# A FiLM layer on one core: slab 0 stored in five parts and loaded in two, and a small write of zeros left out

## The chip, the cores and the metric

The kernel runs on one core of a Trainium2 chip. The metric is device time in microseconds (us), the median of several runs; the kernel before takes 84.38 us (three runs, 84.28 to 84.4). A profile shows one execution. Its "span" runs from the first to the last instruction of the program, and its own time is a little longer than its span.

## The reference

```python
batch, seq, dim = 32, 512, 256
cond_dim = 64
...
    gamma = conditioning @ gamma_proj
    beta = conditioning @ beta_proj

    return (x * (1 + gamma[:, None, :]) + beta[:, None, :]).astype(np.float32)
```

All is float32. x and the output have 32 x 512 rows of 256 values, 1 KB a row and 16 MB each (16.78 million bytes). Every batch element has one row of gamma and one of beta, which are used for its 512 rows.

## The kernel before

**Tiling.** The 16384 rows are cut into four slabs of 4096 rows (SLABS, L29). In a slab each of the 128 partitions holds 32 rows that follow one another in memory (ROWS, L32), so a partition's share of a slab is one run of 32 KB, and 16 partitions share one batch element (REP). All four slabs fit in SBUF at once (tiles xs0 to xs3, L62), and nothing is loaded twice or waits for a buffer.

**Loads.** SyncE (SP) issues them all (L66): slab 0 in four DMAs of 8 rows (LOADS, L38), each of which moves 8 KB per partition, slabs 1 to 3 in one DMA each, 32 KB per partition. ScalarE (ACT) issues the small ones: conditioning (L49), then a write of zeros, then gamma_proj and beta_proj (L57, L58) into the even and odd rows of one tile, gbproj.

**The write of zeros.** POOL fills a tile of 16 rows with zeros (L52), and ACT issues one DMA (L54) which writes them to rows 0, 1024, 2048 and so on of the output: one row in each MB. The stores of the results write over them later.

**The coefficients.** VectorE widens conditioning into two tiles (L83, L84); TensorE multiplies each by an identity matrix that repeats every batch element 16 times (L74, L86), which transposes it; VectorE copies the result out of PSUM (L89). For each slab two matmuls with gbproj (L96) give gamma and beta for all partitions in PSUM (gb_p), and ACT copies them to SBUF (gb_s, L100 and L103), adding the 1 to gamma. VectorE reads them from PSUM, POOL, from SBUF.

**The arithmetic.** The loop (L110 to L127) goes over slabs and over two groups of 16 rows in each (GROUP). In a group VectorE takes the first 11 rows of a partition (ON_DVE) and POOL the other 5. Each makes one multiplication and one addition in place (L118 and L121 on VectorE, L120 and L122 on POOL).

**The stores.** ACT issues them (L126). STORES (L39) lists the rows up to which a store reaches: slab 0 in two halves of 16 rows, the others whole. The inner loop (L124) issues, behind each group, every store that ends in that group.

**The order.** The framework makes the semaphores and keeps each engine's instructions in an order of its own that follows the program. Loads stand on SP's queue (q1 in the profile), stores and the small DMAs on ACT's (q10). Both queues run on the same 16 DMA engines. Each DMA reports its end on one of the completion semaphores.

Of the kernel before, what the change touches and what calls it, by code (L numbers as in the profile page):

```python
# [2 lines left out]

# [5 lines left out]


@with_exitstack
def kernel(
    ctx: ExitStack,
    tc: tile.TileContext,
    x: bass.AP,
    conditioning: bass.AP,
    gamma_proj: bass.AP,
    beta_proj: bass.AP,
    out: bass.AP,  # L20
):
    nc = tc.nc
    f32 = mybir.dt.float32
    ALU = mybir.AluOpType

    batch, seq, dim = x.shape
    cond_dim = conditioning.shape[1]
    P = 128
    SLABS = 4  # L29
    BS = batch // SLABS  # L30
    REP = P // BS
    ROWS = BS * seq // P  # L32
    assert SLABS * BS == batch and REP * BS == P and ROWS * REP == seq

    x_v = x.flatten_outer_dims().rearrange("(s p r) d -> s p r d", s=SLABS, p=P)
    o_v = out.flatten_outer_dims().rearrange("(s p r) d -> s p r d", s=SLABS, p=P)

    LOADS = {0: [8, 8, 8, 8]}  # L38
    STORES = {0: (16, 32), 1: (32,), 2: (32,), 3: (32,)}  # L39
    GROUP = 16  # L40
    ON_DVE = 11

    consts = ctx.enter_context(tc.tile_pool(name="consts", bufs=1))
    xpool = ctx.enter_context(tc.tile_pool(name="xpool", bufs=1))
    psum = ctx.enter_context(tc.tile_pool(name="psum", bufs=1, space=bass.MemoryType.PSUM))


    cond_s = consts.tile([batch, cond_dim], f32)
    nc.scalar.dma_start(out=cond_s, in_=conditioning)  # L49

    zero = consts.tile([16, dim], f32)
    nc.gpsimd.memset(zero, 0.0)  # L52
    o_f = out.flatten_outer_dims()
    nc.scalar.dma_start(out=o_f.rearrange("(a b) d -> a b d", a=16)[:, 0, :], in_=zero)  # L54

    gbproj = consts.tile([2 * cond_dim, dim], f32)
    nc.scalar.dma_start(out=gbproj[0::2, :], in_=gamma_proj)  # L57
    nc.scalar.dma_start(out=gbproj[1::2, :], in_=beta_proj)  # L58

    slabs = []  # L60
    for s in range(SLABS):
        xs = xpool.tile([P, ROWS, dim], f32, name=f"xs{s}")  # L62
        slabs.append(xs)
        r = 0
        for n in LOADS.get(s, [ROWS]):
            nc.sync.dma_start(out=xs[:, r : r + n, :], in_=x_v[s, :, r : r + n, :])  # L66
            r += n
        assert r == ROWS


    ident = consts.tile([batch, batch], f32)
    make_identity(nc, ident)
    rident = consts.tile([batch, batch * REP], f32)
    nc.vector.tensor_copy(  # L74
        out=rident.rearrange("p (b g) -> p b g", g=REP),
        in_=ident.to_broadcast([batch, batch, REP]),
    )


    cond_T = []  # L80
    for h in range(2):
        wide = consts.tile([batch, cond_dim, 2], f32, name=f"wide{h}")
        nc.vector.memset(wide, 0.0)  # L83
        nc.vector.tensor_copy(out=wide[:, :, h], in_=cond_s)  # L84
        t_p = psum.tile([2 * cond_dim, batch * REP], f32, name=f"cond_T_p{h}")
        nc.tensor.matmul(t_p, lhsT=wide.rearrange("b k h -> b (k h)"), rhs=rident,  # L86
                         start=True, stop=True)
        t_s = consts.tile([2 * cond_dim, batch * REP], f32, name=f"cond_T{h}")
        nc.vector.tensor_copy(out=t_s, in_=t_p)  # L89
        cond_T.append(t_s)  # L90

    gb_p, gb_s = [], []
    for s in range(SLABS):
        p_t = psum.tile([P, 2 * dim], f32, name=f"gb_p{s}")
        for h in range(2):
            nc.tensor.matmul(p_t[:, h * dim : (h + 1) * dim],  # L96
                             lhsT=cond_T[h][:, s * P : (s + 1) * P], rhs=gbproj,
                             start=True, stop=True)
        s_t = consts.tile([P, 2 * dim], f32, name=f"gb_s{s}")
        nc.scalar.activation(out=s_t[:, :dim], in_=p_t[:, :dim],  # L100
                             func=mybir.ActivationFunctionType.Identity,
                             bias=1.0, scale=1.0)
        nc.scalar.copy(out=s_t[:, dim:], in_=p_t[:, dim:])  # L103
        gb_p.append(p_t)
        gb_s.append(s_t)

    def rows(t, n):
        return bass.AP(tensor=t.tensor, offset=t.offset, ap=[t.ap[0], [0, n], t.ap[1]])

    for s in range(SLABS):  # L110
        xs = slabs[s]
        g_p, b_p = gb_p[s][:, :dim], gb_p[s][:, dim:]
        g_s, b_s = gb_s[s][:, :dim], gb_s[s][:, dim:]
        for r0 in range(0, ROWS, GROUP):
            v = xs[:, r0 : r0 + ON_DVE, :]
            w = xs[:, r0 + ON_DVE : r0 + GROUP, :]
            nv, nw = ON_DVE, GROUP - ON_DVE
            nc.vector.scalar_tensor_tensor(out=v, in0=rows(g_p, nv), scalar=1.0, in1=v,  # L118
                                           op0=ALU.add, op1=ALU.mult)
            nc.gpsimd.tensor_tensor(out=w, in0=w, in1=rows(g_s, nw), op=ALU.mult)  # L120
            nc.vector.tensor_add(out=v, in0=v, in1=rows(b_p, nv))  # L121
            nc.gpsimd.tensor_tensor(out=w, in0=w, in1=rows(b_s, nw), op=ALU.add)  # L122

            for e0, e1 in zip((0,) + STORES[s], STORES[s]):  # L124
                if r0 < e1 <= r0 + GROUP:
                    nc.scalar.dma_start(out=o_v[s, :, e0:e1, :], in_=xs[:, e0:e1, :])  # L126
        assert STORES[s][-1] == ROWS  # L127


# [1 line left out]
_INS = ['x', 'conditioning', 'gamma_proj', 'beta_proj']  # L131
_OUTS = [((32, 512, 256), 'float32')]


# [23 lines left out]
```

## Time and profile before

| what | us |
|---|---|
| median of 3 runs | 84.38 |
| the profiled execution | 84.28 |
| its span | 82.5 |
| VectorE busy | 51.2 |
| POOL busy | 46.5 |
| TensorE busy | 9.0 |
| DMA queue q1 (loads), share of 16 engines' span | 48.7% |
| DMA queue q10 (stores and small DMAs), the same | 47.8% |

The DMAs of x, from the trace: when each was issued, and when the last of its 16 engines reported its end.

| DMA | issued | landed |
|---|---|---|
| slab 0, load, rows 0, 8, 16, 24 on | 0.75, 1.17, 1.64, 2.11 | 5.7, 8.4, 10.9, 13.4 |
| slab 1, load | 4.10 | 23.1 |
| slab 2, load | 6.35 | 36.9 |
| slab 3, load | 9.94 | 51.4 |
| slab 0, store, rows 0 to 15 | 22.10 | 40.5 |
| slab 0, store, rows 16 to 31 | 26.09 | 52.6 |
| slab 1, store | 38.34 | 62.3 |
| slab 2, store | 50.58 | 72.0 |
| slab 3, store | 63.93 | 81.7 |

How to read it: a busy engine is not yet the one that bounds the time. The time from a DMA's issue to its landing holds its stand in the queue as well as its transfer. The profile's slices, each a fortieth of the span, show in tenths how busy an engine was. The trace also has a record of each DMA packet, with its queue, size, start and duration; some records of the small end markers are doubled.

### The profile page before, as it was taken

The numbers are of one execution on the slowest core, as the hardware profiler recorded it, in microseconds if no ns is written. First come the engines' busy times: TensorE is split into PE (matmuls) and PEld (weight loads), VectorE is DVE, ScalarE is ACT, GpSimd is POOL, SyncE is SP. The second block draws the span as 40 slices with busy tenths as digits, with TensorE's granted clock in tenths as the row PEclk, the third lists the DMA queues.
The fourth block names the chain that finished last, engine by engine and source line by source line (L and its number), as shares of the span: only waits on it lengthen the run. The fifth ranks groups of instructions, "written<-read, shape, count | busy, mean of one in ns | idle before, by whom it ended". The sixth has DMA issues, their size and how long they took to land.

```text
span 82.5 us, 179 instructions
## 1 busy us (share of the span) xinstructions
PE 9.0 (11%) x20; PEld 5.2 (6%) x20; DVE 51.2 (62%) x23; ACT 3.8 (5%) x9; POOL 46.5 (56%) x23
## 2 busy tenths in 40 slices
PE   0069399300000000000000000000000000000000
PEld 0031178100000000000000000000000000000000
DVE  1023303999999999999999995999999000000000
ACT  0500005600000000000000000000000000000000
POOL 3000004999999999969999940999995000000000
PEclk9999999998555555555555555555555555555555
DMA  3799999989979999999899988979997995998890
GB/s 52 298 425 419 427 437 560 413 350 508 477 302 413 477 477 397 381 493 397 350 413 461 556 381 350 540 334 429 508 445 318 508 508 254 508 508 381 381 508 0
DMA packets 1968, 33.71 MB, mean 409 GB/s; under 512 B 288, under 2 KB 432, under 8 KB 432
## 3 DMA queue, kind: packets, MB, share of 16 engines
q1 hardware_dynamic: 1008, 16.78, 48.7%
q10 hardware_dynamic: 960, 16.93, 47.8%
HBM read 16.92 MB, written 16.79 MB: 409 GB/s over the span
## 4 chain that ended last, share of the span: by engine, by line
DMA 60%; DVE 15%; ACTq 1%; issue 1%; POOL 0%; DVEq 0%; POOLq 0%
DMA xs<-in_x_dram 50%; DMA gbproj<-in_beta_proj_dram 9%; DVE xs L121 7%; DVE xs L118 7%; ACTq L57 1%; ACTq L54 0%; POOL ident masks.py:199 0%; POOL ident masks.py:197 0%; POOL zero L52 0%; DVEq L118 0%; POOLq L142 0%
## 5 line engine op out<-in xcount | busy, mean ns | idle before, releaser
L120 POOL TENSOR_TENSOR xs<-xs,gb_s 128x1280 f32<-128x1280 f32 x8 | 23.0, 2897 | 15.9 <-ACT gb_s L100 12.1
L118 DVE SCALAR_TENSOR_TENSOR xs<-gb_p,xs 128x2816 f32<-128x2816 f32 x8 | 24.7, 3085 | 5.3 <-ACT gb_s L103 4.3
L121 DVE TENSOR_TENSOR xs<-xs,gb_p 128x2816 f32<-128x2816 f32 x8 | 24.7, 3087 | 0.3
L122 POOL TENSOR_TENSOR xs<-xs,gb_s 128x1280 f32<-128x1280 f32 x8 | 23.0, 2898 | 0.0
L96 PE MATMUL gb_p<-gbproj,cond_T 128*128 128x256 f32 x16 | 5.2, 494 | 1.4 <-DMA gbproj<-in_beta_proj_dram 1.4
L86 PE MATMUL cond_T_p<-rident,wide 32*128 32x512 f32 x4 | 3.8, 1096 | 4.9 <-DVE rident L74 4.9
L96 PEld LDWEIGHTS gb_p<-gbproj,cond_T 128*128 128x128 f32 x16 | 4.0, 261 | 3.7 <-DVE cond_T L89 3.0
L89 DVE COPY cond_T<-cond_T_p 128x512 f32<-128x512 f32 x2 | 1.4, 692 | 3.2 <-PE cond_T_p L86 3.2
L84 DVE COPY wide<-cond_s 32x64 f32<-32x64 f32 x2 | 0.3, 181 | 3.0 <-DMA cond_s<-in_conditioning_dram 3.0
L100 ACT ACTIVATE gb_s<-gb_p 128x256 f32<-128x256 f32 x4 | 1.5, 383 | 9.2 <-PE gb_p L96 9.2
L86 PEld LDWEIGHTS cond_T_p<-rident,wide 32*128 32x128 f32 x4 | 1.2, 318 | 5.9 <-DVE rident L74 4.8
L103 ACT COPY gb_s<-gb_p 128x256 f32<-128x256 f32 x4 | 1.5, 367 | 0.0
L100 ACT ACT_TABLE_LOAD x1 | 1.3, 1283 | 2.9 <-issue 2.9
L83 DVE MEMSET wide<- 32x128 f32 x2 | 0.3, 165 | 0.8 <-PEq L142 0.8
L52 POOL MEMSET zero<- 16x256 f32 x1 | 0.3, 301 | 0.3 <-POOLq L142 0.3
L74 DVE COPY rident<-ident 32x512 f32<-32x512 f32 x1 | 0.4, 407 | 0.0
masks.py:199 POOL TENSOR_SCALAR_AFFINE_SELECT ident<-ident 32x32 f32<-32x32 f32 x1 | 0.2, 202 | 0.1
L142 POOL MEMSET const-float32-0.0<- 128x1 f32 x1 | 0.1, 103 | 0.2 <-issue 0.2
masks.py:197 POOL MEMSET ident<- 32x32 f32 x1 | 0.1, 114 | 0.0
L142 POOL MEMSET const-bfloat16-1.0<- 128x1 bf16 x1 | 0.1, 111 | 0.0
L142 POOL MEMSET const-uint8-127<- 128x1 uint8 x1 | 0.1, 111 | 0.0
L142 POOL MEMSET const-float32-1.0<- 128x1 f32 x1 | 0.1, 108 | 0.0
## 6 DMA issues: line engine op xcount, KB each, us to landing
xs<-in_x_dram SPq DMA_DIRECT2D x3, 4096.0 KB, 30.5
out_dram<-xs ACTq DMA_DIRECT2D x3, 4096.0 KB, 21.4
xs<-in_x_dram SPq DMA_DIRECT2D x4, 1024.0 KB, 8.3
out_dram<-xs ACTq DMA_DIRECT2D x2, 2048.0 KB, 22.5
gbproj<-in_gamma_proj_dram ACTq DMA_DIRECT2D x1, 64.0 KB, 6.8
gbproj<-in_beta_proj_dram ACTq DMA_DIRECT2D x1, 64.0 KB, 7.7
cond_s<-in_conditioning_dram ACTq DMA_DIRECT2D x1, 8.0 KB, 3.3
out_dram<-zero ACTq DMA_DIRECT2D x1, 16.0 KB, 5.1
```

What stands on the lines that cost most here:

```text
L57: nc.scalar.dma_start(out=gbproj[0::2, :], in_=gamma_proj)
L74: nc.vector.tensor_copy(out=rident.rearrange("p (b g) -> p b g", g=REP), in_=ident.to_broadcast([batch, batch, REP]),)
L86: nc.tensor.matmul(t_p, lhsT=wide.rearrange("b k h -> b (k h)"), rhs=rident, start=True, stop=True)
L89: nc.vector.tensor_copy(out=t_s, in_=t_p)
L96: nc.tensor.matmul(p_t[:, h * dim : (h + 1) * dim], lhsT=cond_T[h][:, s * P : (s + 1) * P], rhs=gbproj, start=True, stop=True)
L100: nc.scalar.activation(out=s_t[:, :dim], in_=p_t[:, :dim], func=mybir.ActivationFunctionType.Identity, bias=1.0, scale=1.0)
L103: nc.scalar.copy(out=s_t[:, dim:], in_=p_t[:, dim:])
L118: nc.vector.scalar_tensor_tensor(out=v, in0=rows(g_p, nv), scalar=1.0, in1=v, op0=ALU.add, op1=ALU.mult)
L120: nc.gpsimd.tensor_tensor(out=w, in0=w, in1=rows(g_s, nw), op=ALU.mult)
L121: nc.vector.tensor_add(out=v, in0=v, in1=rows(b_p, nv))
L122: nc.gpsimd.tensor_tensor(out=w, in0=w, in1=rows(b_s, nw), op=ALU.add)
L142: nc = _bacc.Bacc("TRN2", target_bir_lowering=False, num_devices=1)
```

## The change

Four edits. The tile of zeros and its DMA go. Slab 0 is loaded by two DMAs, of 8 and 24 rows. The loads get a limit on the length of one run of a DMA: 8 KB for slab 0, 32 KB (the whole of a partition's share) for the others. Slab 0 is stored in five parts, which end at rows 2, 4, 8, 16 and 32; the first four are issued behind group 0, the last behind group 1.

```diff
-    LOADS = {0: [8, 8, 8, 8]}
-    STORES = {0: (16, 32), 1: (32,), 2: (32,), 3: (32,)}
+    LOADS = {0: [8, 24]}
+    RUN = {0: 8}
+    STORES = {0: (2, 4, 8, 16, 32), 1: (32,), 2: (32,), 3: (32,)}
...
-    zero = consts.tile([16, dim], f32)
-    nc.gpsimd.memset(zero, 0.0)
-    o_f = out.flatten_outer_dims()
-    nc.scalar.dma_start(out=o_f.rearrange("(a b) d -> a b d", a=16)[:, 0, :], in_=zero)
-
...
-            nc.sync.dma_start(out=xs[:, r : r + n, :], in_=x_v[s, :, r : r + n, :])
+            nc.sync.dma_start(out=xs[:, r : r + n, :], in_=x_v[s, :, r : r + n, :],
+                              max_dma_last_dim=RUN.get(s, ROWS) * dim * 4)
```

## The prediction

> **What bounds the kernel now.** I read four views: the page's slices, its chain of work, the waits of the DMA queues, and the span cut into windows.
>
> The slices come first. Rows: busy tenths of VectorE, of the DMA engines, and what these moved.
>
> ```profile
> DVE  1023303999999999999999995999999000000000
> ...
> DMA  3799999989979999999899988979997995998890
> GB/s 52 298 425 419 427 437 560 413 350 508 477 302 413 477 477 397 381 493 397 350 413 461 556 381 350 540 334 429 508 445 318 508 508 254 508 508 381 381 508 0
> ```
>
> The DMA row is at 7 or more from the second slice to the last but one (the single 5 lies among slices whose bytes were booked to a neighbour), while VectorE stops nine slices before the end. The kernel is a copy through 16 DMA engines with arithmetic beside it. The queue rows say so once more: 48.7 and 47.8%, together 96.5% of 16 engines' span.
>
> ```profile
> q1 hardware_dynamic: 1008, 16.78, 48.7%
> q10 hardware_dynamic: 960, 16.93, 47.8%
> ```
>
> The chain of work would mislead: it names 50% "DMA xs<-in_x_dram" and then VectorE from 51.5 to 63.9 us. It follows what released what, and so ends in the compute of slab 3, but the store which that compute releases (issued at 63.93) has to stand behind the store of slab 2.
>
> The windows show where the engines are not at their pace (columns after the stretch: its length, VectorE's busy time and count, granted clock, DMA share, GB/s):
>
> ```profile
> 0.00:2.00 2.00, 0.31 (x2) 1.00 0.31 45
> 2.00:4.00 2.00, 0.00 (x0) 1.00 0.82 299
> ...
> 28.00:34.00 6.00, 5.97 (x3) 0.50 1.01 434
> 34.00:36.00 2.00, 1.97 (x2) 0.50 1.03 401
> 36.00:50.00 14.00, 13.93 (x5) 0.50 1.00 431
> ```
>
> Packet by packet the trace says the same. A load or store packet of 32 KB took 1.213 us, one of 16 KB 0.611, one of 8 KB 0.309, one of 1 KB 0.046, and the 4-byte packet that ends a DMA 0.009; from 4 us on an engine starts one within 10 ns of the end of the one before. The first packet starts at 1.74 us and the last ends at 81.33. Of these 79.6 us the start costs 0.61 (the first packets of 8 KB took up to 1.24; their excess over 0.309, summed and divided by 16). Three short stalls cost 0.54: load packets begun at 24.7 to 25.2 took up to 1.84 instead of 1.213 (0.30 a engine), those begun at 26.8 to 27.0 up to 1.38 (0.04), and those at 34.2 to 34.6 up to 1.54 (0.20). So nearly the whole time is bytes at full pace, and only what changes the packets, or a stall, changes the end.
>
> **The change, part by part.** The sum is made against the profiled execution: 84.28 us, of which 82.5 are span and 1.78 lie around it. The median is 84.38, 0.10 above.
>
> *The zeros.* One packet of 1 KB and one end marker per engine go: 0.046 + 0.009 = -0.055 us. POOL's memset (0.30) and ACT's issue (0.44, with its wait) go too; gamma's and beta's issues move up by about 0.48. The zeros' two packets each stood in turn with a load packet of 8 KB, so beta lands 2 x 0.355 = 0.7 us sooner, 9.2 instead of 9.93. The matmuls of L96 can start only when cond_T is copied (9.35, against 10.06 now), so VectorE could start at 13.0 instead of 13.68.
>
> *Loads of slab 0.* The packets stay 32 of 8 KB per engine, since the 24 rows are cut into 8 KB runs; two end markers go, -0.02 us. Rows 8 to 31 now land together: the fourth load landed at 13.4, so group 0 (rows 0 to 15) waits until about 13.3 where it had its rows at 8.4. VectorE starts at 13.3 to 13.4, 0.3 us earlier than now.
>
> *Slots of the loads.* The queue's own waits show loads of x waiting for DMAs that they share no data with:
>
> ```profile
> SPq L66 <- DMA gbproj<-in_beta_proj_dram: 3.3, 1, 3.3
> SPq L66 <- DMA out_dram<-zero: 1.9, 1, 1.9
> SPq L66 <- DMA cond_s<-in_conditioning_dram: 1.3, 1, 1.3
> ```
>
> The trace has eight completion semaphores; the ninth, tenth and eleventh DMA wait for one to come free. Three small ones and five loads make eight, so all loads are out by about 3.5 us instead of 9.94. It is worth nothing: slab 0 kept the load queue full until 13.0. The eight stores then take the eight semaphores over. A store held by a late load's semaphore would stand behind slab 3's landing at worst, and would only change the order in which a full set of engines moves the same bytes.
>
> *Stores of slab 0.* Rows 0 to 7 need VectorE alone (row 11 is the first of POOL's), so three parts could go out at 19.6 rather than 22.1. In packets, eight per engine and part: 2, 2, 4, 8 and 16 KB. The trace has no 2 or 4 KB packet. Between 1 KB (45 ns a KB) and 8 KB (38.6 ns a KB), 2 KB lies in 0.077 to 0.092 and 4 KB in 0.154 to 0.184; the straight line through the rows (8 ns plus 36.8 ns a KB) gives 0.083 and 0.158. Sum: 8 x (0.083 + 0.083 + 0.158 + 0.309 + 0.611) = 9.95 us against 16 x 0.611 = 9.78: +0.17, bounds +0.05 and +0.53. Three end markers: +0.03.
>
> The Trainium skill ("DMA: Bandwidth & Descriptors", Rules for kernel authors, and its fit under Anatomy of one DMA) speaks against this part: it wants at least 1 MiB in a DMA and gives each a fixed cost of about 2 us, an estimate of 6 us for three more stores if each cost stood alone. The row decides here: on engine 0 the end marker of slab 0's first store is at 40.025 and a load packet follows at 40.031, with the next store's first packet in its turn; a DMA that is queued behind another in good time costs its 9 ns.
>
> *Order of the bytes.* Where both queues have work an engine takes one packet of each in turn (32 KB in, 16 KB out, 1.83 us a pair, from 26 to 50 us). A 2 KB store packet then gets 2 KB per turn: a pair is 1.30 us. With the first store packet at about 23.4 (issue plus the 3.7 us that the first one took from the end of its issue to its first packet) some 15 load packets per engine are left, which all pair with 2 KB packets: the loads end at 23.4 + 15 x 1.30 = 43, not 51. The stores that did not go out by then follow, and the end does not move, if the store queue never runs dry. It doesn't: after 43 the rest of slab 0 needs 8.7 us, to 52; slab 1 is computed at 38, slab 2 (wanted at 61.7) at 50.5, slab 3 (wanted at 71.4) at 13.4 + 8 x 6.19 = 62.9. Less 3.7 us to the first packet, 4.8 us are left. VectorE's wait for slab 3 (1.02 us) goes into this reserve, as do the 0.3 us above.
>
> Sum: -0.055 - 0.02 + 0.17 + 0.03 = +0.13 us, bounds 0.0 and +0.48; 84.41 beside the profiled execution, 84.51 beside the median.
>
> **The stalls** are the term that I cannot work out. The first two stand around the first packets of slab 0's first store; the third follows its fifth (on engine 0 that store packet began at 33.837 and the next load packet took 1.339). An engine's first four packets lie in one MB of the output and the next four in the following: each stall comes where an engine enters a new MB with data. Slab 0's second store, into the same MBs, has none; nor have the stores of slabs 1 to 3. The zeros had been written to each of these MBs at 5.1 to 5.5, and no load packet beside them took over 0.32. So either the zeros help and slab 0 pays something else, or they don't and the stall belongs to loads and stores starting to mix. I keep 0.54 in the forecast, as the row stands.
>
> **Rivals.**
>
> *The zeros kept slabs 1 to 3 free of stalls.* Then without them an engine stalls at its first and fifth packet of each slab's first store. For: the stalls sit at MB entries, and slabs 1 to 3 show none. Against: slab 0's MBs had their zeros too, and stalled. Price: 3 x 0.54 = +1.6 us, 84.51 + 1.62 = 86.1, slower. It decides from about 0.02 us a stall on (six of them reach 0.2% with the sum above), since from 43 us nothing else runs that could hide it.
>
> *The stalls go.* If they come from 16 KB packets meeting loads all at once, 2 KB packets in turn with 1.2 us loads give 25 GB/s of stores in place of 140. For: the first packets of a phase stall, later ones don't; the load queue's start does the same. Against: the third stall comes 7.6 us after the start. Price: -0.54: 83.97, faster.
>
> *The cut into 8 KB doesn't happen, or the small DMAs come later.* With runs of 24 KB (0.91 us) gamma's and beta's ten turns take 9.6 us, beta lands near 15, VectorE starts at 18.9, past the reserve (13.4 + 4.8 = 18.2): up to +0.8, 85.3. For: no packet of that kind is in the trace. Against: 32-row loads show that the packet follows the run, 32 KB.
>
> **How the numbers follow.** A measurement of this kernel can tell about 0.2% (0.17 us). Forecast, 0.42: 84.5, own range 84.3 to 84.9; 0.32 of it within 0.2%, 0.10 slower. Zeros mattered, 0.20: slower. Stalls go, 0.26: 0.23 faster, 0.03 within. Compute late, 0.06: slower. The rest, 0.06, half faster, half slower. Faster 0.26, same 0.35, slower 0.39. The range reaches from the third case to the second, 83.9 to 86.2.
>
> **What would show it.** Right: DMA share near 1.00 from 4 to 80 us; slab 3 landing near 44 us instead of 51.4; no SyncE waits at L66; VectorE never waiting for slab 2 or 3; the last packet at about 81.4. Wrong: load or store packets over 1.22 us after 45 us (the zeros), none over 1.22 between 20 and 40 (stalls gone), VectorE starting after 18, or a store queue empty between 52 and 80.

## The result and the profile after

The kernel after takes 84.73 us (median of 6 runs, 84.61 to 84.86), the kernel before 84.33 in the same comparison (84.22 to 84.4): a ratio of 1.0048, 95% interval 1.0035 to 1.0062. The change costs 0.40 us. The forecast was 84.5, +0.13 on the kernel before; the forecast's own range, 84.3 to 84.9, and the whole range, 83.9 to 86.2, hold the result.

The profiled execution of the kernel after took 84.67 us, 82.9 of them span. The rows of its slices, as in the prediction: VectorE, the DMA engines, what they moved.

```profile
DVE  1023305999999999999999999999991000000000
...
DMA  3799999979979969899699999989988998998890
GB/s 55 308 433 422 434 411 534 506 316 443 506 338 468 538 269 538 356 451 538 269 271 405 439 451 427 553 364 411 506 380 380 506 474 380 411 506 380 380 506 0
```

VectorE has lost the dip that it had in the middle (a 5 in the 25th slice before), and ends 1.4 us earlier: slab 3 lands at 44.5 us instead of 51.4, and nothing waits for it. The DMA row still runs to the end. The queues carry the same bytes (less the zeros) in more packets, and all that were added are on the stores' side:

```profile
q1 hardware_dynamic: 976, 16.78, 48.8%
q10 hardware_dynamic: 1360, 16.92, 47.8%
```

Where the time went shows in four windows of the kernel after (columns: length, VectorE busy and count, granted clock, DMA share, GB/s):

```profile
14.00:22.00 8.00, 7.97 (x3) 0.88 0.93 401
22.00:40.00 18.00, 17.90 (x7) 0.50 1.01 431
40.00:44.00 4.00, 3.96 (x2) 0.50 0.93 310
52.00:80.00 28.00, 10.40 (x4) 0.50 1.01 434
```

The engines are booked as busy for 93% or more of each window, but from 40 to 44 us they moved 310 GB/s where they move 431 to 434 before and after. (A window books a packet whole, so short windows at either end of a phase are a little off.) In the packet records this is one stall: all 16 load packets begun at 41.7 to 42.0 took 1.69 to 2.09 us instead of 1.213, and eight begun at 40.2 to 40.5 up to 1.67. Summed and divided by 16 that is 0.82 us an engine. The three stalls before, at 24.7, 26.8 and 34.2, made 0.54, and of them nothing is left: while 2 KB store packets go in turn with loads, from 23.4 to 40 us, no packet is late.

The books of the two profiled executions, 84.67 - 84.28 = +0.39 us. "Mean end" is the mean over the 16 engines of the time at which the end marker of slab 3's store starts; "behind" is by how much the slowest engine is later than that mean; "rest" is from there to the execution's own time.

| | mean end | behind | rest | time |
|---|---|---|---|---|
| before | 81.17 | 0.15 | 2.96 | 84.28 |
| after | 81.45 | 0.26 | 2.96 | 84.67 |

Of the +0.28 in the mean end, +0.13 is the packet sum of the prediction, +0.28 the larger stall, -0.06 a slightly better start (0.55 us lost there in place of 0.61); -0.07 I cannot place. The other +0.11 is the slowest engine, a term that the prediction did not have.

### The profile page after: what moved, and what is told of

Same layout as the page of the kernel before. It is cut to its first block, busy times and chain, and to the rows that moved or that the text cites. A ratio compares the mean times of both kernels' runs of the same rounds, so it can differ in the third digit from the quotient of the medians.

```text
span 82.9 us, 178 instructions
## 1 busy us (share of the span) xinstructions
PE 9.2 (11%) x20; PEld 5.4 (6%) x20; DVE 51.1 (62%) x23; ACT 3.9 (5%) x9; POOL 46.2 (56%) x22
## 4 chain that ended last, share of the span: by engine, by line
DVE 48%; issue 11%; DMA 10%; PE 4%; ACTq 1%; ACT 1%
DVE xs L115 29%; DVE xs L118 19%; DMA gbproj<-in_beta_proj_dram 10%; PE gb_p L93 4%; ACTq L53 1%; ACTq L50 0%; ACT gb_s L97 0%; ACT gb_s L100 0%
## 5 line engine op out<-in xcount | busy, mean ns | idle before, releaser
L115 DVE SCALAR_TENSOR_TENSOR xs<-gb_p,xs 128x2816 f32<-128x2816 f32 x8 | 24.7, 3082 | 4.2 <-ACT gb_s L100 4.2
L118 DVE TENSOR_TENSOR xs<-xs,gb_p 128x2816 f32<-128x2816 f32 x8 | 24.7, 3086 | 0.3
```

## The experiments

Two theories stood at the outset. **A:** a stall belongs to a fixed meeting of loads and stores. **B:** it comes from outside, at any time. When A fell, **F** took its place: the stall comes once, the first time that stores flow at a high rate, and is the larger the bigger that step. Beside them stood the prediction's rival that the zeros matter. "Lost" is what packets after the first 3 us took over their usual time, summed and divided by 16, from the trace.

**The kernel before again** (no edit).

> The kernel before, unchanged, for a second trace and for the noise. All theories: within 0.1% of itself. Theory A (a stall belongs to a fixed meeting of loads and stores): the three stalls stand again at 24.7, 26.8 and 34.2 us, 0.54 us an engine. Theory B (a stall comes from outside at any time): they stand elsewhere or are of another size.

Ratio 0.9996 (0.9979 to 1.0014). The stalls stood at 24.6 to 25.1 (0.47 us), 26.8 to 27.1 (0.01) and 34.1 to 34.5 (0.11): 0.60 in all, in the same places, though each had another size (0.30, 0.04 and 0.20 before). Their places belong to the program, so B falls; their sizes differ from one execution to the next.

**Without the zeros.**

```diff
-    zero = consts.tile([16, dim], f32)
...
-    nc.scalar.dma_start(out=o_f.rearrange("(a b) d -> a b d", a=16)[:, 0, :], in_=zero)
```

> The kernel before without the zeros and nothing else. Packets alone: -0.055 us, ratio 0.9993, all packets of the stores of slabs 1 to 3 at 1.213 us. The rival that the zeros matter: stalls at the first and fifth packet of those stores, up to +1.6 us, ratio 1.019; or, for a smaller part of the result, about half of the +0.40.

Ratio 1.0006 (0.9988 to 1.0023); mean end 81.10, 0.07 before that of the kernel before, which is the 0.055 of the packets within what two traces differ. The stalls (0.60) came at 22 to 29.5 us, with the store's issue, which was 1.0 us earlier; every store packet of slabs 1 to 3 took 1.213. The zeros keep nothing free of stalls.

**The five parts alone.**

```diff
-    STORES = {0: (16, 32), 1: (32,), 2: (32,), 3: (32,)}
+    STORES = {0: (2, 4, 8, 16, 32), 1: (32,), 2: (32,), 3: (32,)}
```

> The kernel before with slab 0 stored in five parts and nothing else. Packets alone: +0.20 us, ratio 1.0024, with the stalls as before. Theory A, with the stalls moved by the change of turns to the end of the loads: +0.4 to +0.5 us, ratio 1.005 to 1.006, load packets near 41 us of up to 2 us as in the kernel after.

Ratio 1.0115 (1.0089 to 1.0141): more than the whole change, and more than either theory gave. The stall stood at 40.2 to 42.3, 0.88 us. The mean end moved by 0.41, about what 0.23 of packets and end markers and 0.34 of stall less 0.1 at the start make. The rest, about 0.9 of the profiled 1.3, is behind the mean: 0.57 for the slowest engine (0.72 behind the mean, where it was 0.15) and 0.32 after the last packet. Both are taken up below.

**The two loads alone.**

```diff
-    LOADS = {0: [8, 8, 8, 8]}
+    LOADS = {0: [8, 24]}
+    RUN = {0: 8}
...
+                              max_dma_last_dim=RUN.get(s, ROWS) * dim * 4)
```

> The kernel before with slab 0 loaded by two DMAs in 8 KB runs and nothing else. Packets alone: -0.02 us, ratio 1.000. If the later landing of slab 0's first half or another order of the loads matters for the end: +0.1 us or more, and the order of the issues at the load line changes.

Ratio 1.0015 (0.9997 to 1.0033): nothing that could be told from none. Stalls in the old places, 0.67 us.

**One queue for loads and stores**, on which stores follow loads and the two never take turns.

```diff
-                    nc.scalar.dma_start(out=o_v[s, :, e0:e1, :], in_=xs[:, e0:e1, :])
+                    nc.sync.dma_start(out=o_v[s, :, e0:e1, :], in_=xs[:, e0:e1, :])
```

> The kernel before with all stores of results on SP's queue, behind the loads, so that loads and stores never take turns. Theory A (the stalls belong to the meeting of the two queues): no load packet over 1.22 us after 3 us, the loads end near 41.5, the last packet ends near 80.8: -0.5 us, ratio 0.994. Rival (a stall belongs to the first stores, whichever queue they stand on): store packets over 1.22 us near 41 to 46, ratio 1.000. A second thing to see: without stalls nothing evens the engines out, and the slowest keeps its lag of the start (0.3 to 0.5 us), which would eat half of the gain.

Ratio 1.0044 (1.003 to 1.0059), and theory A falls: without any turns the stall is the largest of all, 0.98 us, on the loads' last two packets per engine (39.1 to 41.2), just ahead of the first store packets. The windows of this kernel, columns as above:

```profile
22.00:38.00 16.00, 15.89 (x6) 0.50 0.99 428
38.00:43.00 5.00, 4.96 (x3) 0.50 1.01 351
52.00:80.00 28.00, 10.52 (x4) 0.50 1.01 436
```

Full pace with loads alone, full pace with stores alone, 351 GB/s at the change from one to the other.

**Parts of 2 and 30 rows** in the kernel after.

```diff
-    STORES = {0: (2, 4, 8, 16, 32), 1: (32,), 2: (32,), 3: (32,)}
+    STORES = {0: (2, 32), 1: (32,), 2: (32,), 3: (32,)}
```

> The kernel after with slab 0 stored in parts of 2 and 30 rows: 2 KB packets in turn with loads from 22 to 32.5 us, then 30 KB packets from 33 us while slab 3 is still loading. If the stall comes when large store packets first join the loads: load packets of up to 2 us at 30 to 34 us, about 0.5 to 0.8 us an engine, none at 40 to 42. If it belongs to the issue of slab 1's store at 38 us: again at 40 to 42. If it belongs to 2 KB packets beside the loads' last ones: none at all, ratio 0.998.

Ratio 1.0067 (1.0045 to 1.0089). The stall moved to 31.2 to 35.6 (0.59 us), just ahead of the first 30 KB packets, and none stood at 40 to 42 on the loads, nor on their last packets, which began at 50.6. So the end of the loads alone does not bring a stall. Another 0.32 was spread over 30 KB store packets at 41 to 50 us. So 2 KB packets don't set the stall off, and the first large ones do, wherever they come. The profiled execution was 0.85 longer than that of the kernel before: 0.24 of mean end, 0.43 of the slowest engine and 0.18 after the last packet.

**Two halves again** in the kernel after: it differs from the kernel before by the zeros and the loads.

```diff
-    STORES = {0: (2, 4, 8, 16, 32), 1: (32,), 2: (32,), 3: (32,)}
+    STORES = {0: (16, 32), 1: (32,), 2: (32,), 3: (32,)}
```

> The kernel after with slab 0 stored in two halves again: it differs from the kernel before by the missing zeros and the two loads. If the five parts carry the change's cost: ratio 1.000 to 1.002, stalls of about 0.6 us an engine at 22 to 28 us, store ends spread over 0.3 to 0.6 us. If the other two edits carry a part of it together: ratio 1.003 or more.

Ratio 1.001 (1.0002 to 1.0019), against 1.0048 with the five parts: the five parts carry the change's cost. Stalls at 23.4 to 34.5, 0.75 us. This kernel pays 0.22 us more than the kernel after behind the last landing (2.83 against 2.61), for a reason that the last experiment shows.

**Slab 1's store later**, in the kernel after.

```diff
+            if (s, r0) == (2, 0):
+                late = slabs[1][:, ROWS - 1, dim - 1 :]
+                nc.vector.scalar_tensor_tensor(out=late, in0=slabs[2][:, 0, :1], scalar=0.0,
+                                               in1=late, op0=ALU.mult, op1=ALU.add)
+                nc.scalar.dma_start(out=o_v[1], in_=slabs[1])
...
-                if r0 < e1 <= r0 + GROUP:
+                if s != 1 and r0 < e1 <= r0 + GROUP:
```

> The kernel after with slab 1's store held back from 38 to about 47 us by one more VectorE instruction of one column that reads slab 2 (the values stay the same). If the stall at 40 to 42 us follows the issue of slab 1's store: gone there, -0.7 us against the kernel after, ratio to before 0.997, or later and smaller. If it belongs to the end of the loads or to a place in the addresses: it stands at 40 to 42 us with 0.7 to 0.8 us, ratio 1.005 to before.

The store was issued at 47.7 instead of 38.1; the ratio is 1.005 (1.0032 to 1.0068), and the stall stayed, 0.81 us at 40.2 to 42.0. The same windows as for the kernel after:

```profile
22.00:40.00 18.00, 17.89 (x7) 0.50 1.01 431
40.00:44.00 4.00, 3.96 (x3) 0.50 0.94 314
52.00:80.00 28.00, 10.86 (x4) 0.50 1.00 432
```

314 GB/s beside 310: what slab 1's store does at 38 us has no part in it.

**Parts of 8, 8 and 16 rows** in the kernel after.

```diff
-    STORES = {0: (2, 4, 8, 16, 32), 1: (32,), 2: (32,), 3: (32,)}
+    STORES = {0: (8, 16, 32), 1: (32,), 2: (32,), 3: (32,)}
```

> The kernel after with slab 0 stored in parts of 8, 8 and 16 rows: the first store packets are of 8 KB, so stores begin at about 85 GB/s beside the loads, where 16 KB gave 140 and 2 KB 25. Theory F (one stall, the first time that stores flow at a rate far above 25 GB/s, the larger the step): the stall stands at 22 to 25 us, 0.3 to 0.6 us an engine, none near 40; ratio 1.000 to 1.003. If 8 KB is still too little: the stall moves to about 35 us, when the 8 KB parts give way to 16 KB ones.

Ratio 1.0029 (1.0007 to 1.0052). The expectation missed the place: 0.10 us at 22 to 27, hardly more at 35, and 0.46 at 43.5 to 45.7, on the loads' last packets. Lost in all: 0.56. The expected switch to 16 KB packets beside the loads never came: the 8 KB packets lasted until 47.5, past the loads' last packets, and the first one of 16 KB began at 46.7. So stores went from 85 GB/s straight to the full rate, and the larger part of the stall stands just ahead of that.

```profile
22.00:26.00 4.00, 3.96 (x3) 0.50 1.08 455
26.00:44.00 18.00, 17.89 (x7) 0.50 1.01 435
44.00:48.00 4.00, 3.96 (x3) 0.50 0.88 328
```

The mean end is 81.19, as good as before; the time is lost behind it (the slowest engine 0.53 behind the mean, and 0.08 more after the last packet). The slowest was already 0.50 behind the mean when slab 0's first load landed.

**Slab 0 stored whole**, no zeros.

```diff
-    STORES = {0: (16, 32), 1: (32,), 2: (32,), 3: (32,)}
+    STORES = {0: (32,), 1: (32,), 2: (32,), 3: (32,)}
```

> The kernel before without the zeros and with slab 0 stored whole: the fewest packets. Packets alone: eight fewer of 8 ns, one end marker, the zeros: -0.13 us, ratio 0.9985. Theory F: one stall at 26 to 30 us, when the 32 KB packets begin, of 0.4 to 0.7 us, so ratio 0.998 to 1.001. If large first packets stall more or spread the engines: 1.002 or more.

Ratio 1.0048 (1.0029 to 1.0067): the fewest packets, and 0.5% slower. The stall, at 26.9 to 30.5, is 0.85 us: 32 KB packets in turn with 32 KB loads begin at 217 GB/s. Beside the kernel before, the mean end is 0.22 later, the slowest engine adds 0.37 and the tail behind the last packet 0.13.

**A megabyte of zeros early**, the test of F.

```diff
+    zero = consts.tile([P, 8, dim], f32)
+    nc.gpsimd.memset(zero, 0.0)
+    nc.scalar.dma_start(out=o_v[0, :, 0:8, :], in_=zero)
```

(It stands behind make_identity, in place of the 16 rows.)

> The kernel before with 1 MB of zeros (8 rows of every partition of slab 0) written at about 3 to 10 us in place of the 16 rows; the results are stored over them later as ever. The megabyte itself is 8 packets of 8 KB an engine: +2.4 us. Theory F: the stall comes with it, load or store packets well over 0.31 us at 4 to 10 us, and none stands at 24 to 34 us any more: +2.3 to +2.6 us, ratio about 1.029. If the stall belongs to where the loads and the result stores meet: 0.5 to 0.6 us at 24 to 34 us as before, and none early. If it belongs to both: +2.9 us or more, ratio 1.035.

Ratio 1.0294 (1.0261 to 1.0328), the number that F gave. A stall left in its old place would have given nearly the same ratio; what tells the cases apart is where the stall stands. First the kernel before in four windows, then this one (columns: length, POOL busy and count, clock, DMA share, GB/s):

```profile
6.00:11.00 5.00, 0.00 (x0) 1.00 1.01 422
14.00:22.00 8.00, 8.00 (x3) 0.87 1.00 430
24.00:30.00 6.00, 6.00 (x3) 0.50 0.88 355
30.00:36.00 6.00, 6.00 (x3) 0.50 1.03 431
```

```profile
6.00:11.00 5.00, 0.00 (x0) 1.00 1.01 350
14.00:22.00 8.00, 7.63 (x3) 0.78 1.08 464
24.00:30.00 6.00, 4.17 (x3) 0.50 1.01 437
30.00:36.00 6.00, 6.00 (x3) 0.50 1.01 434
```

The dip has moved from 24 to 30 us to 6 to 11. The packet records say 0.83 us at 6.3 to 10.5, spread over some 75 packets, and after that not one late packet to the end, though the result stores are issued beside the loads at 22.2 us, as in the kernel before. Here, once stores had flowed at 217 GB/s beside the loads, nothing stalled again.

**The five parts alone, again.**

> The five parts alone a second time: the first run gave +1.1 us, of which its trace explains 0.44 by the mean end of the 16 engines and the rest by one engine that was 0.26 us behind the next from the start and kept it. If that lag is a chance of one start: a trace without a straggler, 84.8 to 85.0 us, ratio 1.004 to 1.006. If it belongs to this kernel: again 85.3 to 85.6, ratio 1.010 to 1.014, with one engine behind from the first packets on. The stall stands at 40 to 42 us with 0.8 to 0.9 us either way.

Ratio 1.0099 (1.0081 to 1.0117). The cost belongs to the kernel, but not in the way that was expected. One engine was again last from the start (it ended slab 0's first load 0.22 us after the next one), but at the end the slowest stood 0.36 behind the mean, not 0.72; the stall was 0.85. Such a lag is not particular to this kernel: with the two loads alone it was 0.35 in the first load. The books against the kernel before: 85.17 - 84.28 = 0.89, of which 0.38 is mean end, 0.21 the slowest engine, and 0.30 comes after the last packet. That last piece shows in SyncE's waits at the end of the program; the kernel before first, then this one:

```profile
SPq L153 <- DMA out_dram<-xs: 33.5, 3, 15.7
SPq L153 <- DMA xs<-in_x_dram: 26.6, 1, 26.6
SPq L153 <- DVE xs L121: 11.1, 1, 11.1
```

```profile
SPq L153 <- DMA out_dram<-xs: 68.5, 1, 68.5
```

At its end SyncE waits for the semaphores of the program one instruction after another, from number 103 up. In the kernel before the last store has number 109, the highest that a DMA has; the earlier waits are done one by one while it is under way. With the five parts alone the last store got 103, SyncE stood at that one wait for 68.5 us, and the other five instructions came after it, 0.06 us each. The list of line 153 (times: first and last start), before and then with the five parts:

```profile
L153 SPq EVENT_SEMAPHORE  x8: 17/28/1536, 36.9 to 82.4; - x8
```

```profile
L153 SPq EVENT_SEMAPHORE  x8: 17/28/28, 82.3 to 83.3; - x8
```

All fourteen traces fit: from the landing of the last store to the execution's time it is 2.60 to 2.62 us with one such instruction left (the kernels before and after among them), 2.67 with two, 2.72 to 2.74 with three, 2.79 to 2.83 with four, 2.91 to 2.92 with six.

## Why the prediction was right, and where it was not

The time came out in the range, 0.22 us above the forecast of 84.5, but the sum gave +0.13 us and the change cost 0.40. The packets in the sum were right; what it missed, a larger stall and a slower last engine, was small beside the range. Nothing in the sum bounded the stall's size, so that it stayed this small was luck.

**The bound: right.** DMA engines at full pace set the time, and only packets and stalls moved it. VectorE ended 1.4 us earlier and slab 3 was issued at 62.55 (62.9 predicted), for nothing.

**Packets: right.** 2 KB took 0.084 us (0.083), 4 KB 0.159 (0.158); slab 0's stores made 9.97 us an engine (9.95). The zeros' 0.055 shows as 0.07 in the mean end when they alone go. The line through the packets is 8 ns plus 37.7 ns for each KB of 1024 bytes; the prediction's 36.8 is for 1000 bytes, but its 0.083 and 0.158 are right. An end marker took 9 ns in the kernel after too. The 2 us a DMA that the prediction set against this part are in the Trainium skill ("DMA: Bandwidth & Descriptors", Anatomy of one DMA) a fit to DMAs that GpSimd issues; ACT issues the stores here.

**Order of the bytes: right.** Turns of one packet each; the loads' last end marker at 44.1 (43), the first 2 KB packet at 23.39 (23.4), the first stores' issue at 19.65 (19.6), no wait of VectorE for slabs 2 and 3. VectorE's start at 13.41 (13.3 to 13.4) was right by luck: it followed ACT's copy of the coefficients, which ended at 13.38, and not slab 0's second load, which landed at 13.16.

**The slots of the loads: wrong, without effect.** I had eight DMAs take eight semaphores, and all loads out by 3.5 us. SyncE still waited, for gamma's and for slab 0's second load:

```profile
SPq L62 <- DMA gbproj<-in_gamma_proj_dram: 5.3, 1, 5.3
SPq L62 <- DMA xs<-in_x_dram: 5.3, 1, 5.3
```

Slabs 2 and 3 were issued at 7.49 and 13.18: the semaphores of gamma's load and of slab 0's second load were used again, while two that the stores took later were still unused. The queue was full all the same. Beta landed at 9.66 instead of 9.2, because one engine had its end marker 0.5 us after the others; it held up the coefficients, but only until 13.38.

**The stalls: the term that failed.** "I keep 0.54 in the forecast, as the row stands" was the wrong size: 0.82. Small first packets did not stall, as the rival "The stalls go" had it, but they did not spare the stall either; they put it off to the loads just ahead of the moment when the stores go from 25 GB/s to everything the engines have. Sizes by the step that set it off: 0.54 to 0.75 us at 140 GB/s beside loads (five traces), 0.83 to 0.85 at 217 (two; with 30 KB packets after 2 KB ones 0.91, a third of it on store packets), 0.81 to 0.88 from 25 to 430 (after, and three traces with the same parts), 0.98 from nothing to 430. With 8 KB first it was 0.56, most of it just ahead of a step from 85 to 430, so the size does not follow from the step alone. In the four traces beside the kernel before with 16 KB first it was 0.60 to 0.75; against these the stall of the kernel after is larger by 0.1 to 0.2 us rather than by 0.28.

**The slowest engine: a term that was missing.** The end is the last of 16 engines, not their mean, and engines differ by 0.3 to 0.8 us from the first packets on. In the kernel before the stall at 24.7 held the early ones longer than the late: the end markers of slab 1's load lie within 0.5 us, those of slab 2's within 0.26. The stall at 41.7 does not even them out: within 0.31 us ahead of it, 0.53 after. Evening out is not sure with 16 KB first either: without the zeros the spread went only from 0.66 to 0.52 us, with the two loads alone from 0.66 to 0.59.

**The rivals.** No part of the zeros shows (ratio 1.0006 without them, 0.9988 to 1.0023). Their rival's threshold of 0.02 us a stall was a slip: with +0.13 in the sum, six stalls of 0.007 us already reach 0.2%. The stalls did not go. The cut into 8 KB took place: 512 load packets of 8 KB, as before.

**What stays open.** Why the first flow of stores costs 0.5 to 1.0 us is not shown: runs moved it in time and in size, but none shows what is waited for. Nearly all late packets are loads, most of them begun before the large stores' first packet (before: from 24.7, against 26.19; after: all of them by 41.99, against 43.58 for the first of 4 KB); the store packets kept their usual time except in the kernel with 2 and 30 rows. That entering a new MB sets it off is out, since in the kernel after 2 KB packets had entered slab 0's without a stall, and the stores of slabs 1 to 3 entered theirs without one. Why the third stall of the kernel before stands apart from the first, at 34.2, I cannot say. None of the versions was faster than the kernel before.

## What to carry to other kernels

Where DMA engines are full from end to end, a smaller first store only moves bytes about: reckon its packets (here 8 ns each over the bytes), the slowest engine and what stands behind the last landing, since the compute it frees is worth nothing. Easing into the first event did not dodge the stall that is tied to it; look at what the first full-rate moment will be after the edit. And compare versions by mean end, slowest engine and tail apart: here 0.3 us of what the five parts alone seemed to cost was only the place of one semaphore in a list.

## What the runs showed of the hardware that was not expected

- The first flow of stores at a rate of 140 GB/s or more cost each DMA engine 0.5 to 1.0 us in all fourteen traces, within 13 us of its first late packet, and nothing in the rest of the execution; only with parts of 2 and 30 rows another 0.32 us followed; a first flow at 85 GB/s cost 0.10. 1 MB of early zeros (8 packets of 8 KB an engine) is enough to have it behind, 16 rows of 1 KB and two whole rounds of 2 KB packets at 25 GB/s are not.
- The packets' durations lie on one line, 8 ns plus 37.7 ns a KB, for loads and stores alike: 1 KB 0.046, 2 KB 0.084, 4 KB 0.159, 8 KB 0.309, 16 KB 0.611, 32 KB 1.213 us.
- Two queues take turns by single packets, whatever their sizes, so 2 KB store packets left the loads 94% of the engines.
- The waits at the end of the program cost 0.06 us apiece when they come after the last landing.
